# A hybrid decoder step on one core: where the sample rows land, how many input tiles wait for their store, and which tiles hold the weights of the first gate/up pass

## The chip, the cores and the metric

The kernel runs on one core of one Trainium2 chip. The metric is the device time of one launch in microseconds; the median of the runs shown is compared before and after.

## The reference, cut to what matters

The prompt (1024 rows of 1024) and 8 sample rows go through one layer with shared weights.

```python
h = rms_norm(x, norm1)
u, q, k, v, ga, gb = split_in(h, w_in, q_norm, k_norm)      # one input projection
y_pool = pool_mix(u_ext, pos, pool_mix_w, pool_scale)       # trailing means over 2/4/8/16 rows
y_attn = sink_attention(qb, kk, vv, mask, sinks)            # window 128, 8 heads, 2 kv heads
x = x + (sigmoid(ga) * (y_pool @ w_pool_proj) + sigmoid(gb) * (y_attn @ w_attn_proj)) @ w_out
h = rms_norm(x, norm2)
x = x + (silu(h @ w_gate) * (h @ w_up)) @ w_down            # 1024 -> 2816 -> 1024
```

Returned are x of both groups, the last 128 keys and values, and the last 15 rows of u. All of it is float32.

## The kernel before, in words

Every matmul is made of three passes of TensorE (PE): each operand is split into a high part (a cast, on ScalarE, L138 or L214) and a low part (a subtraction, on VectorE, L139 or L215), and high x high, high x low and low x high are added in PSUM. The program order within each engine is laid down ahead by a planner, which follows the order of the source text as a priority and takes what its own timeline believes to be ready; on the chip each engine, and the one queue through which SyncE (SP) issues nearly all DMAs, then runs that order without overtaking.

**Input stage.** The 1032 rows (8 sample rows first) are worked in three chunks `CH`. `norm_load` (L298) loads the rows of a chunk, `norm_stats` their sums of squares, `turn` (L335) transposes 128 columns of a chunk on PE and splits the result into `hTh`/`hTl`. Its inner function `keep` (L344) also copies the transposed piece into a tile `xT` and stores that to `xscr` in DRAM, from where the residual is read later. `xT` has six buffers; eight pieces belong to a chunk. `norm_bc` (L364) copies the row factors of a chunk (`bc1`) out of PSUM on ScalarE; `do_k`, `do_v` and `do_q` need them as soon as their matmuls are done (`kr`, L390). The sample rows stand in a tile `xs` of their own in the pool `st`. The keys have four units of 4128 bytes a partition in the pool `kp`: `Kh` and `Kl` for two key heads; half of each `Kl` is zeroed on GpSimd (POOL) at the start.

**First gate/up pass.** The feed-forward part works on halves of rows and columns with seven products instead of eight (`strassen`, L1138): products 1, 6, 2, 7, 5, 4, 3, each with an operand of activations (`c1h` to `c7l`, made by `combos`, L1049, for a quarter set s = 0 or 1) and one of weights. Block p = 0 of the weights is done twice: for s = 0 alone right after the output projection `out_proj(1, m)` (n = 0 in the last loop of the pass), while the second norm and the `combos` of s = 1 are being made, and for s = 1 alone at the end (n = 11). Between them p = 1 to 10 take both s. The seven weight operands of gate p = 0 were split earlier and lie in DRAM (`wscr`); those of up p = 0 lie there unsplit (`tscr`, or the weights themselves) and are split by `wparts` when their product is due. A product of n = 0 is 12 matmuls, one of n = 1 is 24.

Where these operands are put: `kept_gate` (L1236) places sets 0 to 4 in the `whi`/`wlo` tiles of the pool `wp` (four buffers each, shared with every other split weight, so also with `out_proj`) and sets 5 and 6 in units of the pool `u1` (28 units of 4128 bytes, which also hold `Mh`/`Ml` of the output projection and all `c` operands). `kept_up` (L1250) places raws 0 to 2 in units of `u1` and raws 3 to 6 in `wtemp` tiles (three buffers, shared with `wraw`). The fifth split of up goes to a tile of its own (pool `mw`). `wide` (L997) gives four wide tiles of 1024 columns, used by `out_proj` for `x2` and by `wblocks` (L1110) for the raw weights of p = 1 onwards. `mark["load"]` is a load behind which other loads are queued on SP: before, the raws of up p = 1 stand behind the load of up raw 2.

The two generators are run from the loop at the end of the pass:

```python
for i, _ in enumerate(chain(strassen(wblocks(wg_v, 2 * P * p) if p else kept_gate(0 if n else 5), streams, g),
                            strassen(wblocks(wu_v, 2 * P * p, mark["load"] if n == 1 else None) if p else kept_up(), streams, u_))):
    if n == 0 and i in (1, 3, 4, 5, 6, 7, 8, 9, 10):
        next(norm)
```

After the pass `down` follows: `srcs` (L1283) loads the products of gate and up back into units of `u1` (`ar`) and splits them.

Of the kernel before, what the change touches and what calls it, by code (L numbers as in the profile page):

```python
# [7 lines left out]
F32 = mybir.dt.float32  # L8
F32R = mybir.dt.float32r
# [7 lines left out]
P = 128  # L17
NS = 8
# [14 lines left out]
HALF = ((slice(0, 64), slice(64, 128)), (slice(64, 128), slice(0, 64)))  # L33
# [3 lines left out]
def hybrid_step(tc, x_prompt, x_sample, cache_k, cache_v, state_pool, norm1, w_in, q_norm, k_norm, sinks,  # L37
# [4 lines left out]
    V, A, G, T, SP = nc.vector, nc.scalar, nc.gpsimd, nc.tensor, nc.sync  # L42
# [12 lines left out]
    wp, wp_es = pool("wp")  # L55
# [86 lines left out]
    mark = {}  # L142
# [109 lines left out]
    def unit(p, name, dt=F32):  # L252
        return p.tile([P, NT], dt, tag="u", name=name)
# [14 lines left out]


    Kh = [unit(kp, f"Kh{kv}", F32R) for kv in range(2)]  # L270
    Kl = [unit(kp, f"Kl{kv}", F32R) for kv in range(2)]
    for kv in range(2):
        G.memset(Kl[kv][HALF[kv][1]].bitcast(F32), 0.0)
    VV = kvp.tile([P, 8, 4, 64], F32R, name="VV")
    st, st_es = pool("st", side="right")

# [21 lines left out]
    def norm_load(c):  # L298
        tiles = []
        if c == 0:  # L300
            xt = st.tile([NS, 1024], F32, name="xs")
            SP.dma_start(xt, x_sample[:, 0])
            tiles.append((NS, 0, xt))
        for i, b in enumerate(CB[c]):
            xt = unit(u1, "xr")
            for q in range(2):
                w = 512
                SP.dma_start(xt[:, w * q:w * q + w], x_prompt[0, b * P:(b + 1) * P, w * q:w * q + w])
            tiles.append((P, (NS if c == 0 else 0) + P * i, xt))
        return tiles  # L310
# [24 lines left out]
    def turn(c, tiles, k):  # L335
        c0, N = CH[c]
        pt = bank("pt")
        for n, off, xt in tiles:
            T.transpose(pt[:, off:off + n], xt[:n, k * P:(k + 1) * P], ident[:n, :n])
        hi, lo = hTh[k][:, c0:c0 + N], hTl[k][:, c0:c0 + N]  # L340
        turned[c, k] = (A.activation(hi, pt[:, :N], AF.Copy, scale=g1[k]),
                        V.scalar_tensor_tensor(lo, pt[:, :N], g1[k], hi.bitcast(F32), ALU.mult, ALU.subtract))

        def keep(e=A):  # L344
            xT = st.tile([P, 384], F32, tag="xT", bufs=6, name="xT")[:, :N]
            if e is A:
                A.copy(xT, pt[:, :N])
            else:
                V.tensor_copy(xT, pt[:, :N])
            SP.dma_start(xscr[:, k, c0:c0 + N], xT)  # L350

        return keep
# [11 lines left out]
    def norm_bc(c, rstd):  # L364
        c0, N = CH[c]
        pb = bank("pb")
        spread_of(c, rstd, pb)
        A.copy(bc1[:, c0:c0 + N], pb[:, :N])
# [63 lines left out]
    def do_v(ws, c):  # L432
        N, nb, o = CH[c][1], len(CB[c]), (NS if c == 0 else 0)
        b0 = CB[c][0]
        ps = group(ws, hTh, hTl, c, bank("pv"))

        def rest():
            vr = t512("vr")[:, :N]
            V.tensor_mul(vr, ps, bc_of(c))

            def token_major():
                pt = bank("pvt")
                for i in range(nb):
                    T.transpose(pt[:, i * P:(i + 1) * P], vr[:, o + i * P:o + (i + 1) * P], ident)
                if c == 0:
                    T.transpose(pt[:NS, 384:512], vr[:, :NS], ident)
                vb = VV[:, b0:b0 + nb]
                split(vb[:, :, 0:4:3], vb[:, :, 1:3], pt[:, :nb * P].rearrange("p (b g d) -> p b g d", g=2, d=64))
                if c == 0:
                    V.tensor_copy(vst, pt[:NS, 384:512])  # L450
                    SP.dma_start(new_v_sample[0, :, 127].rearrange("b h d -> b (h d)"), vst)
                if CB[c][-1] == 7:
                    nv = t512("nv")[:, :P]
                    V.tensor_copy(nv, pt[:, (nb - 1) * P:nb * P])
                    SP.dma_start(new_v_prompt[0, 0].rearrange("t h d -> t (h d)"), nv)

            tick()
            defer(token_major)

        return rest  # L460
# [59 lines left out]
        wv = wsplit2(rv, V)  # L520
    with behind(0, 7):
        norm_bc(0, rs[0])
    ev = do_v(wv, 0)
    ek()
    ev()
# [336 lines left out]
    raw = wraw()  # L862
# [131 lines left out]
        XG.append(p.tile([P, 2, KD, NQ], F32, name=f"xg{s}"))  # L994
        acc.append(p.tile([P, 2, NQ], F32, name=f"acc{s}"))

    def wide(name):  # L997
        return mw.tile([P, 1024], F32, tag="raw", bufs=4, name=name)

    def out_proj(s, m):  # L1000
        ws = wload(wo_v, 0, 8, P * m)
# [75 lines left out]
    def chain(*gens):  # L1077
        for g in gens:
            yield from g
# [19 lines left out]
    def wparts(src):  # L1099

        if nth[0] is None:
            return wsplit(src, 4)
        nth[0] += 1
        return wsplit(src, 4) if nth[0] % 5 else wsplit(src, 4, p=mw, bufs=1)

    def wtemp(name):
        return wp.tile([P, 4, P], F32, tag="wraw", bufs=3, name=name)
# [125 lines left out]


    norm = chain(norm_scale(1), combos(1, hc[1]))
    def kept_gate(early):  # L1236

        for i in range(7):
            if i < early:
                r = [wp.tile([P, 4, P], F32R, tag=t, bufs=4, name=t) for t in ("whi", "wlo")]  # L1240
                for a in range(2):
                    SP.dma_start(r[a].bitcast(F32), wscr[i][:, a])
                yield r
            else:
                u = unit(u1, "wk", F32R)
                SP.dma_start(u[:, :1024].bitcast(F32), wscr[i].rearrange("p a k c -> p (a k c)"))
                u = u[:, :1024].rearrange("p (a k c) -> p a k c", a=2, k=4)
                yield u[:, 0], u[:, 1]

    def kept_up():  # L1250
        for i, (kh, m) in enumerate(((0, 0), (0, 0), (1, 0), (0, 0), (0, 0), (0, 0), (1, 1))):
            raw = unit(u1, "wk")[:, :512].rearrange("p (k c) -> p k c", k=4) if i < 3 else wtemp("wk")
            load = SP.dma_start(raw, tscr[i] if i in tscr else wu_v[:, 4 * kh:4 * kh + 4, P * m:P * m + P])
            if i == 2:
                mark["load"] = load
            yield wparts(raw)

    for n, (p, streams) in enumerate([(0, [0])] + [(p, [0, 1]) for p in range(1, 11)] + [(0, [1])]):
        g = Gate()
        u_ = Up(g)  # L1260
        for i, _ in enumerate(chain(strassen(wblocks(wg_v, 2 * P * p) if p else kept_gate(0 if n else 5), streams, g),
                                    strassen(wblocks(wu_v, 2 * P * p, mark["load"] if n == 1 else None) if p else kept_up(), streams, u_))):
            if n == 0 and i in (1, 3, 4, 5, 6, 7, 8, 9, 10):
                next(norm)
        if n == 0:
            for _ in norm:
                pass
        save(p, g.g, slice(streams[0], streams[-1] + 1))
        if n == 1:
            m0_es.close()  # L1270
            xb_es.close()
            m1, m1_es = pool("m1", bufs=16, side="right")
            mt[0] = m1
# [162 lines left out]
    a = {}  # L1436
# [56 lines left out]
```

## Time and profile before

| what | before |
|---|---|
| median of 3 runs | 1282.99 us (1282.97 to 1284.46) |
| profiled execution | 1284.43 us |
| its span in the trace | 1282.7 us |
| PE busy | 1248.0 us, 97% |
| VectorE (DVE) busy | 817.3 us, 64% |
| ScalarE (ACT) busy | 501.4 us, 39% |
| mean DMA rate | 120 GB/s |

A busy share of 97% says that PE is what the span is made of; what is left to find are the few stretches in which it stands, and those in which its clock is granted at half. PE, PEld, DVE, ACT, POOL are engines, SPq is the queue on which SP issues DMAs. In rows of the timeline the bracket at the end is the idle time of the engine before the instruction, with what ended it.

### The profile page before, as it was taken

The page shows a single profiled execution, that of the slowest core. Times are in us where ns is not written, and L with a number is a line of the kernel's source. Part 1 is how long each engine was busy: PE and PEld are TensorE (multiplying, and loading weights), DVE is VectorE, ACT ScalarE, POOL GpSimd, SP SyncE. Part 2 cuts the span into 40 slices and gives each one's busy share as a digit, 9 for nine tenths or more (in the row PEclk, how much of TensorE's full clock was granted, in tenths as well). Part 3 has the DMA queues.
Part 4 walks back from the last instruction along what each step waited for, and adds up shares of the span by engine and source line. Part 5 has one row for each costly group of instructions (what it writes and reads, how often), then busy time and mean ns, then how long its engine had stood idle before and what let it go on. Part 6 is the DMA issues. An engine that isn't in the chain of part 4 may idle for free.

```text
span 1282.7 us, 23784 instructions
## 1 busy us (share of the span) xinstructions
PE 1248.0 (97%) x9436; PEld 1233.9 (96%) x9436; DVE 817.3 (64%) x1600; ACT 501.4 (39%) x980; POOL 55.9 (4%) x193
## 2 busy tenths in 40 slices
PE   5999999999999999996999999999999999999997
PEld 5999999999999999996999999999999999999997
DVE  5769788585353484487756566665666566878642
ACT  5747555451233234454323232232322234334433
POOL 3213211000000000000000000000000000000000
PEclk7999999999999999998999999999999999999999
DMA  7411101211244125664232323322232668847404
GB/s 241 132 46 51 42 23 53 73 51 51 74 157 123 42 83 158 175 187 164 79 125 83 91 87 113 108 93 91 84 124 75 210 222 293 290 156 240 147 26 125
DMA packets 149166, 153.50 MB, mean 120 GB/s; under 512 B 15207, under 2 KB 116263, under 8 KB 149031
## 3 DMA queue, kind: packets, MB, share of 16 engines
q1 hardware_dynamic: 148959, 150.71, 37.1%
q8 instruction: 74, 1.21, 0.4%
q0 software_dynamic: 96, 1.27, 0.2%
q14 instruction: 37, 0.30, 0.1%
HBM read 114.02 MB, written 39.20 MB: 119 GB/s over the span
## 4 chain that ended last, share of the span: by engine, by line
PE 93%; DMA 4%; DVE 2%; SPq 0%; ACT 0%; issue 0%; ACTq 0%; DVEq 0%
PE py L1132 5%; PE py L1134 5%; PE py L1133 5%; PE pg L211 5%; PE pg L209 5%; PE pg L210 5%; PE pz L1132 3%; PE pz L1133 3%; PE px L1134 3%; PE pz L1134 3%; PE px L1132 3%; PE px L1133 3%; PE dy L1132 2%; PE pw L209 2%; PE dy L1133 2%; PE dy L1134 2%
## 5 line engine op out<-in xcount | busy, mean ns | idle before, releaser
L209 PE MATMUL pg<-hTh,whi 128*128 128x384 f32 (+1 forms) x384 | 123.6, 322 | 0.0
L210 PE MATMUL pg<-hTl,whi 128*128 128x384 f32 (+1 forms) x384 | 123.3, 321 | 0.0
L211 PE MATMUL pg<-hTh,wlo 128*128 128x384 f32 (+1 forms) x384 | 122.9, 321 | 0.0
L139 DVE TENSOR_TENSOR wlo<-wraw,whi 128x512 fp32r<-128x512 f32 x102 | 70.1, 687 | 69.6 <-ACT whi L138 62.3
L138 ACT CAST whi<-wraw 128x512 fp32r<-128x512 f32 x102 | 63.0, 619 | 131.2 <-PE pa L210 31.3
L138 ACT CAST whi<-t 128x512 fp32r<-128x512 f32 x80 | 49.4, 621 | 153.8 <-PE py L1133 79.0
L138 ACT CAST whi<-raw 128x512 fp32r<-128x512 f32 x60 | 37.3, 621 | 114.7 <-PE px L1133 66.0
L1132 PE MATMUL dy<-ah,whi 128*128 128x258 f32 x264 | 75.1, 285 | 0.0
L1133 PE MATMUL dy<-al,whi 128*128 128x258 f32 x264 | 75.0, 284 | 0.0
L1134 PE MATMUL dy<-ah,wlo 128*128 128x258 f32 x264 | 74.8, 284 | 0.0
L209 PEld LDWEIGHTS pg<-hTh,whi 128*128 128x128 f32 x384 | 72.6, 189 | 0.6 <-DVE t L823 0.2
L210 PEld LDWEIGHTS pg<-hTl,whi 128*128 128x128 f32 x384 | 72.6, 189 | 0.5
L211 PEld LDWEIGHTS pg<-hTh,wlo 128*128 128x128 f32 x384 | 72.4, 189 | 0.3
L209 PE MATMUL pw<-mh,whi 128*128 128x258 f32 x256 | 72.4, 283 | 0.0
L210 PE MATMUL pw<-ml,whi 128*128 128x258 f32 x256 | 72.1, 282 | 0.0
L211 PE MATMUL pw<-mh,wlo 128*128 128x258 f32 x256 | 72.0, 282 | 0.0
L139 DVE TENSOR_TENSOR wlo<-raw,whi 128x512 fp32r<-128x512 f32 x60 | 41.0, 684 | 35.7 <-ACT whi L138 30.7
L138 ACT CAST whi<-H 128x512 fp32r<-128x512 f32 x55 | 33.8, 620 | 69.0 <-PE dy L1133 23.0
L215 DVE TENSOR_TENSOR al<-ar,ah 128x1032 fp32r<-128x1032 f32 (+1 forms) x42 | 47.9, 1140 | 16.0 <-ACT ah L214 16.0
L139 DVE TENSOR_TENSOR wlo<-t,whi 128x512 fp32r<-128x512 f32 x80 | 54.0, 683 | 3.2 <-ACT whi L138 3.2
L1132 PE MATMUL px<-c1h,whi 128*128 128x258 f32 x172 | 49.3, 286 | 6.1 <-ACT whi L138 6.0
L139 DVE TENSOR_TENSOR wlo<-H,whi 128x512 fp32r<-128x512 f32 x55 | 37.5, 688 | 21.5 <-ACT whi L138 20.4
(446 smaller groups left out, 4451.7 us busy)
## 6 DMA issues: line engine op xcount, KB each, us to landing
ar<-s SPq DMA_DIRECT2D x35, 516.0 KB
d<-in_w_down_dram SPq DMA_DIRECT2D x44, 256.0 KB
s<-g SPq DMA_DIRECT2D x40, 258.0 KB
wraw<-in_w_in_dram SPq DMA_DIRECT2D x40, 256.0 KB
raw<-in_w_gate_dram SPq DMA_DIRECT2D x20, 512.0 KB
raw<-in_w_up_dram SPq DMA_DIRECT2D x20, 512.0 KB
wraw<-in_w_out_dram SPq DMA_DIRECT2D x32, 256.0 KB
s<-fs SPq DMA_DIRECT2D x30, 258.0 KB
```

What stands on the lines that cost most here:

```text
L138: mark["act"] = A.copy(hi, raw)
L139: mark["dve"] = e.tensor_sub(lo, raw, hi.bitcast(F32))
L209: T.matmul(ps, lhsT=wh, rhs=xh, start=(k == 0), stop=False)
L210: T.matmul(ps, lhsT=wh, rhs=xl, start=False, stop=False)
L211: T.matmul(ps, lhsT=wl, rhs=xh, start=False, stop=(k == n - 1))
L215: e.tensor_sub(lo, src, hi.bitcast(F32))
L1132: T.matmul(ps, lhsT=wh, rhs=ah, start=start, stop=False, skip_group_check=True)
L1133: T.matmul(ps, lhsT=wh, rhs=al, start=False, stop=False, skip_group_check=True)
L1134: T.matmul(ps, lhsT=wl, rhs=ah, start=False, stop=stop, skip_group_check=True)
```

## The change

The sample rows `xs` are loaded into a unit of `kp`, the one that the second key head's low part `Kl1` will take; `Kl1` is made (and its half zeroed on POOL) only after the turn of chunk 0. `xT` has eight buffers instead of six. All loads of the first gate/up pass are written out ahead of its loop, in order of need (gate sets 0 to 6, then up raws 0 to 6). Gate sets 0 to 2 stay in `whi`/`wlo`, sets 3 and 4 go to wide tiles, sets 5 and 6 to units. Up raws 0 to 2 go to the small `wtemp` tiles, raws 3 to 6 to units. `mark["load"]` is now the last of these loads, and the gate raws of p = 1 stand behind it too, not only the up raws. In the last pass (n = 11) all seven gate sets and all seven up raws go to units.

```diff
     Kh = [unit(kp, f"Kh{kv}", F32R) for kv in range(2)]
-    Kl = [unit(kp, f"Kl{kv}", F32R) for kv in range(2)]
-    for kv in range(2):
-        G.memset(Kl[kv][HALF[kv][1]].bitcast(F32), 0.0)
+    Kl = []
+
+    def low_keys():
+        Kl.append(unit(kp, f"Kl{len(Kl)}", F32R))
+        G.memset(Kl[-1][HALF[len(Kl) - 1][1]].bitcast(F32), 0.0)
+
+    low_keys()
...
         if c == 0:
-            xt = st.tile([NS, 1024], F32, name="xs")
-            SP.dma_start(xt, x_sample[:, 0])
+            xt = unit(kp, "xs")[:NS]
+            SP.dma_start(xt[:, :1024], x_sample[:, 0])
...
-            xT = st.tile([P, 384], F32, tag="xT", bufs=6, name="xT")[:, :N]
+            xT = st.tile([P, 384], F32, tag="xT", bufs=8, name="xT")[:, :N]
...
     with behind(0, 7):
         norm_bc(0, rs[0])
+    low_keys()
     ev = do_v(wv, 0)
...
-    def wide(name):
-        return mw.tile([P, 1024], F32, tag="raw", bufs=4, name=name)
+    def wide(name, dt=F32):
+        return mw.tile([P, 1024], dt, tag="raw", bufs=4, name=name)
...
-    def kept_gate(early):
-
+    def gate_set(i, where):
+
+        if where == "w":
+            r = [wp.tile([P, 4, P], F32R, tag=t, bufs=4, name=t) for t in ("whi", "wlo")]
+            for a in range(2):
+                SP.dma_start(r[a].bitcast(F32), wscr[i][:, a])
+            return r
+        u = unit(u1, "wk", F32R)[:, :1024] if where == "u" else wide("wk", F32R)
+        mark["load"] = SP.dma_start(u.bitcast(F32), wscr[i].rearrange("p a k c -> p (a k c)"))
+        u = u.rearrange("p (a k c) -> p a k c", a=2, k=4)
+        return u[:, 0], u[:, 1]
+
+    def up_raw(i, small):
+        kh, m = ((0, 0), (0, 0), (1, 0), (0, 0), (0, 0), (0, 0), (1, 1))[i]
+        raw = wtemp("wk") if small else unit(u1, "wk")[:, :512].rearrange("p (k c) -> p k c", k=4)
+        mark["load"] = SP.dma_start(raw, tscr[i] if i in tscr else wu_v[:, 4 * kh:4 * kh + 4, P * m:P * m + P])
+        return raw
+
+    def kept_gate(first):
         for i in range(7):
...
+            yield first[i] if first else gate_set(i, "u")
+
+    def kept_up(first):
+        for i in range(7):
+            yield wparts(first[i] if first else up_raw(i, False))
+
+    first_gate = [gate_set(i, w) for i, w in enumerate("wwwbbuu")]
+    first_up = [up_raw(i, i < 3) for i in range(7)]
...
-        for i, _ in enumerate(chain(strassen(wblocks(wg_v, 2 * P * p) if p else kept_gate(0 if n else 5), streams, g),
-                                    strassen(wblocks(wu_v, 2 * P * p, mark["load"] if n == 1 else None) if p else kept_up(), streams, u_))):
+        for i, _ in enumerate(chain(strassen(wblocks(wg_v, 2 * P * p, mark["load"] if n == 1 else None) if p else kept_gate(None if n else first_gate), streams, g),
+                                    strassen(wblocks(wu_v, 2 * P * p, mark["load"] if n == 1 else None) if p else kept_up(None if n else first_up), streams, u_))):
```

## Rows read from the trace of the kernel before

**Rows 1.** The page: busy time and share of the span, by engine.

```profile
PE 1248.0 (97%) x9436; PEld 1233.9 (96%) x9436; DVE 817.3 (64%) x1600; ACT 501.4 (39%) x980; POOL 55.9 (4%) x193
```

**Rows 2.** Waits of PE, first 60 us: total, times, longest.

```profile
PE pkt L397 <- DVE kr L390: 6.2, 1, 6.2
```

**Rows 3.** The chain that ended last, 22 to 27 us: start, us, what.

```profile
22.24 3.12 DMA xscr<-xT
...
25.70 0.40 ACT bc L368
...
26.12 0.45 DVE kr L390
```

**Rows 4.** Timeline of ACT and DVE, 20 to 26 us: start, us, instruction.

```profile
20.16 0.62 ACT L180 CAST qwh<-qw 128x512 fp32r<-128x512 f32 x1 [1.14 <-DMA qw<-in_w_in_dram]
24.96 0.85 ACT L347 COPY xT<-pt 128x264 f32<-128x264 f32 x2 [4.18 <-DMA xscr<-xT]
...
20.81 0.69 DVE L181 TENSOR_TENSOR qwl<-qw,qwh 128x512 fp32r<-128x512 f32 x1 [1.06 <-ACT qwh L180]
```

**Rows 5.** Stretches: length; busy of PE, PEld, DVE, ACT, POOL; granted clock, DMA, GB/s.

```profile
20.40:26.60 6.20, 0.02 (x1) 0.00 (x0) 1.14 (x3) 1.42 (x4) 0.00 (x0) 0.66 0.88 303
26.60:32.70 6.10, 6.09 (x28) 5.72 (x29) 4.17 (x12) 4.22 (x9) 2.95 (x15) 0.51 0.46 124
```

**Rows 6.** Timeline of POOL: one zeroed half, and the idle time after the first norm.

```profile
4.93 0.95 POOL L273 MEMSET Kl<- 64x1032 f32 x1
...
28.53 0.20 POOL L117 TENSOR_SCALAR rstdk<-rs_v 128x4 int32<-128x4 int32 x1 [15.56 <-DVE rs_v L131]
```

**Rows 7.** Waits of PE, 565 to 620 us: total, times, longest.

```profile
PE px L1132 <- ACT whi L138: 5.4, 1, 5.4
PE pb L1039 <- DVE dg L1034: 2.0, 1, 2.0
```

**Rows 8.** Stretches of the first gate/up pass, 570 to 613 us; columns as in Rows 5.

```profile
570.00:613.00 43.00, 30.81 (x216) 28.72 (x214) 31.99 (x50) 18.76 (x28) 0.00 (x0) 0.88 0.52 171
578.00:588.00 10.00, 6.82 (x61) 6.33 (x60) 3.64 (x15) 2.92 (x4) 0.00 (x0) 1.00 1.03 344
593.00:613.00 20.00, 11.78 (x74) 10.85 (x74) 20.00 (x27) 11.81 (x18) 0.00 (x0) 0.83 0.20 66
601.00:606.00 5.00, 3.96 (x17) 3.64 (x18) 5.00 (x8) 1.82 (x4) 0.00 (x0) 0.50 0.35 108
```

**Rows 9.** Timeline of DVE, 585 to 613 us.

```profile
585.53 0.43 DVE L1164 TENSOR_TENSOR g<-py,g 128x258 f32<-128x258 f32 x1 [1.79 <-PE py L1134]
...
603.01 1.28 DVE L139 TENSOR_TENSOR wlo<-wk,whi 128x512 fp32r<-128x512 f32 x2
...
612.36 0.68 DVE L139 TENSOR_TENSOR wlo<-raw,whi 128x512 fp32r<-128x512 f32 x1
```

**Rows 10.** The chain that ended last, 577 to 584 us: start, us, what.

```profile
577.90 6.08 DMA wlo<-w
```

**Rows 11.** Timeline of PE: first and last matmul of the up pass's last two products.

```profile
615.76 0.28 PE L1132 MATMUL py<-c4h,whi 128*128 128x258 f32 x1
...
618.76 0.28 PE L1134 MATMUL pz<-c3h,wlo 128*128 128x258 f32 x1
```

**Rows 12.** Timeline of SP's queue: a raw of p = 1, an up raw, the down stage's first.

```profile
575.97 0.38 SPq L1114 DMA_DIRECT2D raw<-in_w_gate_dram  x1
...
583.30 0.32 SPq L1253 DMA_DIRECT2D wk<-t  x1
...
1019.33 0.32 SPq L1287 DMA_DIRECT2D ar<-s  x1
```

**Rows 13.** Waits of SP's queue, 535 to 630 us: total, times, longest.

```profile
SPq L1253 <- DVE xg L1067: 19.2, 1, 19.2
```

**Rows 14.** The page's DMA issues: count and size of one.

```profile
raw<-in_w_gate_dram SPq DMA_DIRECT2D x20, 512.0 KB
```

**Rows 15.** Timeline of ACT: cast of the last up raw of the last pass.

```profile
1032.75 0.62 ACT L138 CAST whi<-wk 128x512 fp32r<-128x512 f32 x1
```

More of the change, by code (lines that the diff above doesn't have):

```diff
@@ L1235, in hybrid_step @@
     norm = chain(norm_scale(1), combos(1, hc[1]))
-    def kept_gate(early):
-        for i in range(7):
[L1239 to L1256, printed above, removed]
+    def gate_set(i, where):
[14 more added lines that the diff above has]
+    def kept_gate(first):
+        for i in range(7):
+            yield first[i] if first else gate_set(i, "u")
[4 more added lines that the diff above has]
+    first_up = [up_raw(i, i < 3) for i in range(7)]
     for n, (p, streams) in enumerate([(0, [0])] + [(p, [0, 1]) for p in range(1, 11)] + [(0, [1])]):
```

## The prediction, made before the changed kernel was run

> **What bounds the kernel now.** The page first: PE is busy for 97% of the span [rows 1], so the reader should look for stretches in which PE stands or is granted half its clock. The waits of PE and the table of stretches give two places that this change touches.
>
> The first is the input stage. From 20.4 to 26.6 us PE does nothing: the transposes of the keys wait 6.2 us for `kr` on DVE [rows 2]. The chain tells whom `kr` waited for [rows 3]: for `bc`, a copy on ACT, which stood behind two `xT` copies, and those behind a store of an earlier `xT` that landed at 22.24 + 3.12 = 25.36 us. The timeline of ACT shows the same from the other side: 4.18 us idle, ended by that store [rows 4]. Six buffers, eight pieces to a chunk: pieces 7 and 8 wait for a store that travels among the loads of x (DMA share 0.88 in this stretch). When PE starts again its granted clock is 0.51, the lower of its two levels, 1.2 GHz, nearly up to 32.7 us [rows 5].
>
> The second is the first gate/up pass, 570 to 613 us: PE is busy for 30.8 of 43.0 us, so idle for 12.2 [rows 8], with one wait of 5.4 us for the cast of the up pass's first weights [rows 7]. Two limits follow each other there. At 578 to 588 us the DMA engines are full (1.03, 344 GB/s). From 593 to 613 us nothing is loaded to speak of, and DVE has not a microsecond free (20.00 of 20.00): it makes the s = 1 operands, while the up splits and the additions stand between them [rows 8]. What ends the stretch is a DVE split, that of the first weights of p = 1, at 612.36 + 0.68 = 613.0 us [rows 9].
>
> **Input stage, term A.** With eight buffers all pieces of chunk 0 have one, so both copies run at once after their turn and `bc` no longer stands behind the store. What is late next: on ACT the two casts of `qwh`, the last at 20.16 + 0.62 = 20.78 us, and on DVE the subtraction that ends at 20.81 + 0.69 = 21.50 us [rows 4]. If the order stays, `kr` runs at 21.5 to 21.95 us (0.45, rows 3) and PE goes on at 22.0 instead of 26.6 us: 4.6 us less. The upper end is the whole wait, 6.2 us, if the planner puts `bc` ahead of the casts. The lower end is 1.5 us, if the wait only moves to the copies of chunk 1 (second rival).
> The slow clock afterwards cost 6.1 x (1 - 0.51) = 3.0 us [rows 5]. Whether 1.6 us of idle time still brings it about the trace does not show for this place. The nearest rows are short waits in the gate pass, where 2.0 us [rows 7] lie in the stretch at full clock (578 to 588 us, 1.00), while the stretch behind the 5.4 us wait has 0.50 [rows 8]; short waits can therefore go either way. I take half, 1.5 us, with ends 0 and 3.0. A = 4.6 + 1.5 = 6.1 us. From 30 to 570 us PE has no other wait of this size, so the gain stays in the total.
>
> At nothing: the zeroing of `Kl1`, 0.95 us on POOL, moves from 4.93 us behind the first norm, where POOL idles for 15.56 us [rows 6]; without that cover it would cost its 0.95 us. The load of the sample rows keeps its place and size; its unit is free again once they are turned.
>
> **Gate/up pass, term B.** Three effects, in order.
> (1) Gate sets 3 and 4 no longer need the tiles that the output projection holds. Before, the set of product 7 took 6.08 us to land, at 583.98 us [rows 10]; its product ended late, and DVE, in order, stood 1.79 us before the addition behind it [rows 9] with the rest of the second norm queued there. With the set in place the norm of s = 1, and so DVE's full stretch, starts 1.8 us sooner.
> (2) Up raws 0 to 2 now have small tiles that the output projection frees early, and the `whi` tiles that sets 3 and 4 gave up; raw 3 follows. So four splits can run while DVE is busy for 3.64 of 10 us [rows 8], ahead of the full stretch. A split there takes 1.28 / 2 = 0.64 us [rows 9]: 4 x 0.64 = 2.6 us leave it.
> (3) The up products no longer wait behind DVE. Products 4 and 3 of up, 24 matmuls that came after 613 us, starts 3.0 us apart from first to last with one foreign matmul between [rows 11], or 24 x 0.12 = 2.9 us, are done in time that PE spent idle.
> B = 1.8 + 2.6 + 2.9 = 7.3 us. The low end is effect (1) alone, 1.8 us. The high end is all idle time, 12.2 us, and the half clock of 601 to 606 us, 3.96 x 0.5 = 2.0 us, less the 2.0 us for `dg` that the norm keeps [rows 7, 8]: 12.2 us.
>
> Each queue passed: on SP the gate raws of p = 1, before at 575.97 us, now stand behind the last up raw. Units for six operands come free when the output projection's operands are read; the last up load of before that needed no further unit left at 583.30 us [rows 12]. Add one slow load, 6.1 us [rows 10]: about 590 us, and the split that needs it comes at 613 (613 - 7.3 in the forecast). The cover is over 15 us. Without it: before, SP stood 19.2 us for one up raw's unit [rows 13], until 602.8 us; the raws of p = 1 would land at 608.9, their split end near 610, and B falls from 7.3 to about 5.8.
>
> The last pass (n = 11) asks for four more units than before, just when the down stage wants its first. I cost it at nothing, since the gate sets give back seven units first; the fifth rival has its price.
>
> **Sum.** 6.1 + 7.3 = 13.4 us. Against the profiled execution (1284.43 us, span 1282.7) that is 1271.0; this execution lies 1.44 us above the median of the runs shown, so the median after should be 1282.99 - 13.4 = 1269.6 us.
>
> **The rivals.**
> 1. Bytes decide in the gate pass. DMA stands at 1.03 of its share at 578 to 588 us, so a new order of loads brings nothing, and only the two raws of p = 1 that leave the stretch help: 2 x 512 KB [rows 14] at 344 GB/s = 3.0 us [rows 8]. B = 3.0, sum 9.1: 1273.9 us. For it: that share; against it: before 570 us there is room, and the wide tiles and small tiles open there. The Trainium skill speaks for this rival: "DMA: Bandwidth & Descriptors", section "Issuing engines are not separate DMA queues", says that all DMAs run on the same 16 engines and interleave; by it the sets, pulled forward against each other, only trade places.
> 2. The store's wait moves. Chunk 1's pieces need the buffers of chunk 0 back, whose stores still land from 25.4 us on [rows 3]. If the planner sets the ninth copy ahead of what PE needs, A is 1.5: 8.8 in all, 1274.2 us.
> 3. Both places give their high end: A = 6.2 + 3.0, B = 12.2, 21.4 in all: 1261.6 us.
> 4. It doesn't do what it says: the planner leaves `bc` and the up casts where they are, other waits take over, and the time stays at 1283 us.
> 5. Slower: the down stage starves. If its first load, `ar`, gets a unit only after the last up raw of the last pass is split, it leaves not at 1019.33 us but at 1032.75 + 0.62 + 0.68 = 1034.05 us [rows 9, 12, 15], 14.7 us later. If the stage cannot catch up, PE stands for that and then runs 2.0 us longer at half clock [rows 8]: 16.7 - 13.4 = 3.3 us more than before, 1286.3 us. It decides from about 1030.7 us on (11.4 us late). Against it: the seven gate units are given back one product at a time before that.
>
> **How the numbers follow.** Chances: forecast 0.49, rival 1 0.17, rival 2 0.10, rival 3 0.11, rival 4 0.06, rival 5 0.07. The forecast's own spread is 1265 to 1274. The range runs from rival 3 (1261.6, rounded to 1261) to both low ends together, 1283 - 1.5 - 1.8 = 1279.7, say 1279.5; it leaves out rivals 4 and 5 and a little beside them. A measurement of this kernel tells a change from none at about 0.2%, 2.6 us. Faster by more: forecast and rivals 1 to 3, 0.87; within it 0.06; slower 0.07.
>
> **What the profile after would show.** Right: no wait of PE for `kr` above 2 us and no wait of ACT for `xscr<-xT` before `bc`; in the gate pass four up splits ahead of the multiplication of `xg`, no 5 us wait of `px` for `whi`, and the first p = 1 split on DVE some 13 us earlier than 613 us. Wrong: the wait stands at another copy of `xT`; SP stands long before a load of `wk` or of p = 1; DVE's full stretch is as long as before and PE waits at its end; `dx` waits for `ar`. The forecast fails most easily in effect (3), which needs the planner to put the up products before the operands of s = 1 on PE.

## The result, and the profile after

| what | before | after |
|---|---|---|
| median | 1282.98 us (1282.86 to 1284.46, 4 runs) | 1273.17 us (1270.72 to 1274.98, 4 runs) |
| profiled execution, span | 1284.43 us, 1282.7 us | 1270.72 us, 1268.7 us |
| ratio of the medians | | 0.9919, 95% interval 0.9908 to 0.9931 |

The changed kernel takes 9.8 us less; by the ratio 10.4 us (8.9 to 11.8). A second set of its runs, on another occasion, gave 1273.76 us and 0.9928 (0.9913 to 0.9944). The forecast was 1269.6 us, range 1261 to 1279.5: inside, but 3.6 us too hopeful.

To see where the time went, the start of one and the same matmul is compared in both traces; each number is how many us earlier it starts than before. "Before", "after", "input part" and so on are one profiled execution each.

| landmark (before) | after | after, second profile | input part alone | pass part alone | place of xs alone |
|---|---|---|---|---|---|
| `pk`, first (12.24) | -1.85 | -2.26 | -2.27 | -1.16 | -1.67 |
| `pkt`, first (26.61) | 4.22 | 3.33 | 3.35 | -0.50 | -0.43 |
| `pb` of chunk 1 (39.97) | 6.78 | 6.07 | 6.08 | 0.36 | 0.84 |
| `pg`, first (173.00) | 6.68 | 6.00 | 5.91 | 0.39 | 0.80 |
| `pa`, first (281.86) | 8.25 | 6.01 | 5.92 | 1.94 | 2.38 |
| `pw`, last (577.39) | 8.69 | 6.27 | 6.47 | 2.49 | 1.63 |
| `px` of p = 2, first (650.56) | 11.61 | 6.66 | 6.93 | 4.46 | 1.56 |
| `dx`, first (1041.27) | 12.25 | 7.30 | 7.13 | 5.04 | 1.46 |
| `po`, last (1278.19) | 13.98 | 7.96 | 8.37 | 6.57 | 2.15 |

The input stage gives 5.9 to 6.7 us. Between `pg` and `pa`, where nothing was changed, an execution gains another 1.5 us or none (last section). From the last `pw` to the first `px` of p = 2, the first gate/up pass, the two profiles of the changed kernel gain 2.9 and 0.4 us. From there to the end come 0.6 to 2.4 us more, in kernels without a change there too (1.4 us with the input part alone, 0.6 with the place of xs alone), so they are not counted.

**Input stage.** The waits of PE in the first 45 us after (total, times, longest), the stretches of [rows 5] (the first one from 20.00 us on), and ACT in the timeline:

```profile
PE pt L343 <- DMA xs<-in_x_sample_dram: 3.7, 1, 3.7
...
PE pk L209 <- ACT whi L138: 1.1, 1, 1.1
```

```profile
20.00:26.60 6.60, 6.60 (x55) 6.26 (x54) 5.64 (x16) 4.37 (x10) 1.86 (x10) 1.00 0.94 323
26.60:32.70 6.10, 6.10 (x44) 5.92 (x42) 4.65 (x12) 5.14 (x12) 3.24 (x17) 1.00 0.51 138
```

```profile
20.65 0.62 ACT L180 CAST qwh<-qw 128x512 fp32r<-128x512 f32 x1 [1.10 <-DMA qw<-in_w_in_dram]
21.17 0.38 ACT L351 COPY xT<-pt 128x264 f32<-128x264 f32 x1
21.44 0.39 ACT L372 COPY bc<-pb 128x264 f32<-128x264 f32 x1
...
27.51 0.89 ACT L351 COPY xT<-pt 128x384 f32<-128x384 f32 x2 [1.20 <-DMA xscr<-xT]
```

The wait for `kr` [rows 2] is gone: `bc` runs at 21.44 us behind a copy that waited for no store, PE has no gap from 20 us on, and the clock stays at 1.00 where it was 0.51 [rows 5]. The store is still waited for, now by a copy of chunk 1 and for 1.20 us, and no wait of PE answers to it. The first line has grown: PE stands 3.7 us for the sample rows, before it was 0.7. In return the wait of `pk` for the cast of the key weights fell from 3.8 to 1.1 us. The rows' load left SP second before; after, it leaves fifth, behind three loads of x:

```profile
1.25 1.31 SPq L312 DMA_DIRECT2D xr<-in_x_prompt_dram  x3
2.61 0.33 SPq L306 DMA_DIRECT2D xs<-in_x_sample_dram  x1
```

**First gate/up pass.** The stretches of [rows 8] after, the stretch from 568 to 580 us, and the waits of PE from 560 to 645 us:

```profile
570.00:613.00 43.00, 33.67 (x249) 32.23 (x247) 37.70 (x65) 19.16 (x29) 0.00 (x0) 0.92 0.45 143
578.00:588.00 10.00, 7.00 (x41) 6.60 (x41) 8.85 (x16) 2.27 (x4) 0.00 (x0) 0.83 0.64 192
593.00:613.00 20.00, 14.99 (x106) 14.16 (x104) 20.00 (x33) 9.31 (x14) 0.00 (x0) 0.91 0.24 65
...
568.00:580.00 12.00, 8.67 (x81) 8.47 (x79) 7.64 (x22) 6.12 (x11) 0.00 (x0) 1.00 1.04 356
```

```profile
PE pb L1044 <- DVE dg L1039: 3.8, 1, 3.8
PE px L1137 <- ACT c5h L214: 2.5, 1, 2.5
PE px L1137 <- ACT g L1159: 2.1, 1, 2.1
```

PE's 5.4 us for the first up cast [rows 7] are gone, and the full stretch of the DMA engines lies some 10 us earlier; 8.7 of these are the ones by which the whole pass starts sooner. But PE waits 3.8 instead of 2.0 us for `dg`, and DVE is still full for 20.00 of 20.00 us. DVE's timeline shows what stands ahead of the multiplication of `xg`, with which its full stretch begins:

```profile
575.15 0.16 DVE L131 TENSOR_SCALAR rs_v<-pst 86x6 f32<-86x6 f32 x1 [1.19 <-PE pst L1035]
...
576.87 0.69 DVE L139 TENSOR_TENSOR wlo<-wk,whi 128x512 fp32r<-128x512 f32 x1 [0.96 <-DMA wk<-in_w_up_dram]
...
577.89 0.68 DVE L139 TENSOR_TENSOR wlo<-wk,whi 128x512 fp32r<-128x512 f32 x1
...
579.66 0.69 DVE L1039 TENSOR_TENSOR dg<-ident,rstd 86x516 f32<-86x516 f32 x1
580.46 0.69 DVE L1123 TENSOR_TENSOR t<-raw 128x512 f32<-128x512 f32 x1
581.99 0.69 DVE L1124 TENSOR_TENSOR t<-raw,t 128x512 f32<-128x512 f32 x1 [0.84 <-DMA raw<-in_w_gate_dram]
582.60 0.68 DVE L1128 TENSOR_TENSOR t<-raw 128x512 f32<-128x512 f32 x1
583.20 4.64 DVE L1048 TENSOR_TENSOR xg<-xg,pb 128x1032 f32<-128x1032 f32 x4
```

Two up splits and three sums of p = 1 stand inside the norm's chain, and two of them wait for loads that land in the full stretch of the DMA engines. In the kernel before, the same chain had none of them:

```profile
582.39 0.16 DVE L131 TENSOR_SCALAR rs_v<-pst 86x6 f32<-86x6 f32 x1 [2.74 <-PE pst L1030]
...
588.63 4.65 DVE L1043 TENSOR_TENSOR xg<-xg,pb 128x1032 f32<-128x1032 f32 x4 [1.29 <-PE pb L1039]
```

From the end of the last `pw` matmul (577.67 and 568.99 us), `xg` starts after 11.0 us before and 14.2 us after: 3.2 us later, although the weights of product 7 and of the up pass are there sooner.

### The profile page after: what moved, and what is told of

It reads as the page before. It is cut to its first block, busy times and chain, and to the rows that moved or that the text cites. A ratio compares the mean times of both kernels' runs of the same rounds, so it can differ in the third digit from the quotient of the medians.

```text
span 1268.7 us, 23785 instructions
## 1 busy us (share of the span) xinstructions
PE 1244.1 (98%) x9436; PEld 1229.2 (97%) x9436; DVE 815.5 (64%) x1600; ACT 501.5 (40%) x980; POOL 55.4 (4%) x193
## 4 chain that ended last, share of the span: by engine, by line
PE 92%; DVE 3%; DMA 3%; ACT 1%; issue 1%; SPq 0%; ACTq 0%; DVEq 0%
PE pg L211 5%; PE pg L209 5%; PE pg L210 5%; PE py L1137 5%; PE py L1138 5%; PE py L1139 5%; PE px L1137 3%; PE px L1139 3%; PE pz L1139 3%; PE pz L1138 3%; PE pz L1137 3%; PE px L1138 3%; PE dy L1137 2%; PE dy L1138 2%; PE dy L1139 2%; PE pw L209 2%
## 5 line engine op out<-in xcount | busy, mean ns | idle before, releaser
L139 DVE TENSOR_TENSOR wlo<-wraw,whi 128x512 fp32r<-128x512 f32 x102 | 70.1, 687 | 71.7 <-ACT whi L138 58.6
L209 PE MATMUL pw<-mh,whi 128*128 128x258 f32 x256 | 72.4, 283 | 0.0
L214 ACT CAST ah<-ar 128x1032 fp32r<-128x1032 f32 (+1 forms) x42 | 41.2, 982 | 26.0 <-DMA ar<-s 26.0
```

The lines of the kernel that those rows point to most:

```text
L139: mark["dve"] = e.tensor_sub(lo, raw, hi.bitcast(F32))
L209: T.matmul(ps, lhsT=wh, rhs=xh, start=(k == 0), stop=False)
L214: A.copy(hi, src)
```

## The experiments

The pass is compared by three times, each counted from the end of the last `pw` matmul in the profile of that run; "median" is of the timed runs, "ratio" against the kernel before in the same set.

| run | `rs_v` | `xg` | `px` of p = 2 | median us | ratio [95%] |
|---|---|---|---|---|---|
| before | 4.7 | 11.0 | 72.9 | 1282.98 | 1 |
| e1_input | 4.7 | 10.5 | 72.4 | 1274.98 | 0.9942 [0.9930, 0.9954] |
| e3_xs_only | 4.7 | 10.3 | 73.0 | 1283.34 | 1.0004 [0.9993, 1.0014] |
| after | 6.2 | 14.2 | 70.0 | 1273.17 | 0.9919 [0.9908, 0.9931] |
| a2_again | 6.4 | 15.2 | 72.5 | 1273.76 | 0.9928 [0.9913, 0.9944] |
| e2_pass | 6.2 | 15.1 | 70.9 | 1281.10 | 0.9983 [0.9974, 0.9992] |
| e5_xs_t0 | 6.2 | 15.4 | 72.6 | 1273.58 | 0.9917 [0.9902, 0.9932] |
| e4_behind | 6.2 | 10.8 | 69.1 | 1271.55 | 0.9916 [0.9903, 0.9928] |
| e8_up_units | 4.7 | 11.9 | 69.1 | 1272.82 | 0.9916 [0.9895, 0.9937] |
| e9_pool | 6.2 | 12.8 | 69.8 | 1271.57 | 0.9902 [0.9884, 0.9919] |
| e11_no_lo | 6.2 | 13.0 | 69.7 | 1271.08 | 0.9909 [0.9893, 0.9926] |
| e12_half_sets | 7.2 | 13.0 | 69.7 | 1272.77 | 0.9911 [0.9895, 0.9927] |
| e7_no_wide | 4.9 | 11.6 | 71.8 | 1275.80 | 0.9933 [0.9917, 0.9949] |
| e13_units_behind | 4.7 | 14.0 | 71.7 | 1276.14 | 0.9944 [0.9930, 0.9957] |

### The two parts apart

The input part alone: the hunks of the diff on `Kl`, `xs` and `xT`, in the kernel before.

> The input stage's part of the change alone (sample rows in a key unit, eight xT buffers), the gate/up pass as before. Theory: the trace of the changed kernel stands 8.1 us ahead at the first matmul of the output projection, all of it from the input stage and the clock behind it; so this kernel is 8.1 us faster than before, about 1275, with the pass and the tail unmoved. Rival: the input stage gives only the 4.2 us by which the transposes of the keys came earlier, and the rest is the clock of single executions: then about 1279.

It gave 1274.98 us: by the ratio 7.4 us (5.9 to 9.0). The time is the one that the theory named, but not the share of 8.1 us: this run's profile stands 5.9 us ahead at `pg` and 6.5 at the last `pw`. The rest of the 8.1 was the 1.5 us that the first profile of the changed kernel gained between `pg` and `pa`. The forecast's 6.1 us for this stage lies in the interval.

The pass part alone: the changed kernel with those hunks taken back.

> The gate/up pass's part alone, the input stage as before. Theory: the pass stands 3.5 us ahead by the first product of p = 2 (11.6 ahead, of which 8.1 from the input stage) and the down stage adds up to 2.3 us through the last pass's places: 3.5 to 5.8 us faster, 1277 to 1279.5. Rival: the prediction's size for this part, 7.3 us, hidden in the full change by something else: then about 1275.7.

By the ratio 2.2 us (1.0 to 3.3), against 7.3 forecast; theory and rival were both too hopeful. The two parts add up to 9.6 us, beside 10.4 and 9.2 for the whole. So the forecast's surplus lies in the pass.

The place of the sample rows alone, in the kernel before:

```diff
-            xT = st.tile([P, 384], F32, tag="xT", bufs=8, name="xT")[:, :N]
+            xT = st.tile([P, 384], F32, tag="xT", bufs=6, name="xT")[:, :N]
```

(against the run of the input part)

> The sample rows in a key unit, but xT still with six buffers, the pass as before. Theory: the gain of the input stage is the two buffers alone, and moving the sample rows costs about 1.9 us at the start, since their load now leaves SP behind three loads of the prompt (first key matmul 14.1 instead of 12.2 us): PE still waits some 4 to 6 us for kr, and the time is 1283 to 1285. Rival: the new place itself changes the order on ACT, and the wait is gone with six buffers too: about 1276.

1.0004: no difference. Its waits of PE show the old one back beside the new one:

```profile
PE pkt L401 <- DVE kr L394: 3.7, 1, 3.7
PE pt L343 <- DMA xs<-in_x_sample_dram: 3.6, 1, 3.6
```

Behind that wait the clock is 0.72 from 26.6 to 32.7 us, with eight buffers 1.00. The gain of the stage, the clock's part included, is that of the two buffers.

### The sample rows' load early again

```diff
-            xt = unit(kp, "xs")[:NS]
+            xt = unit(t0p, "xs")[:NS]
```

> The whole change, but the sample rows are loaded into a unit of the pool t0p, so that no later key waits on them and their load need not come behind the three loads of xr. Theory: in the changed kernel that load leaves SP fifth, at 2.61 us instead of 1.25, and this is why the keys of chunk 0 start 1.85 us later (14.09 instead of 12.24 us). Put back, it leaves second, the wait of 3.7 us of the transposes for the rows goes, pk starts near 12.3 us, and the whole input stage gains 1.2 to 1.9 us more: about 1271.5 us. Rival: the keys are bound by something else on their way (the copies of xT on ACT, kr), so that what is won at 12 us is lost again by 22 us: pkt starts at 22.4 us as in the changed kernel, and the time stays at 1273.2 us.

The rival came true. The wait for the rows shrank to 0.6 us and another took its place:

```profile
PE pk L209 <- ACT whi L138: 3.9, 1, 3.9
```

`pk` started at 13.29 instead of 14.09 us, and `pkt` at 22.70 instead of 22.39. What PE waits for next is the key weights' cast and then `kr`, and `kr` (22.22 us here, 21.91 after) stands behind the second cast of `qw`, which starts when its load has landed, at 20.95 us here and 20.65 after. So the late load of the rows costs nothing that can be measured.

### What stands ahead of the second norm

The sums of p = 1 and the splits of up raws 3 to 6 held on DVE behind the multiplication:

```diff
-            V.tensor_mul(x, x, pb[:, t, :NQ].unsqueeze(1).broadcast_to([P, 4, NQ]))
+            mark["xg"] = V.tensor_mul(x, x, pb[:, t, :NQ].unsqueeze(1).broadcast_to([P, 4, NQ]))
...
-        V.tensor_sub(t1, b12, b11)
-        V.tensor_sub(t2, b22, t1)
+        with tc.issue_after(mark["xg"].ins):
+            V.tensor_sub(t1, b12, b11)
+            V.tensor_sub(t2, b22, t1)
...
-        V.tensor_sub(t3, b22, b12)
+        with tc.issue_after(mark["xg"].ins):
+            V.tensor_sub(t3, b22, b12)
...
-            yield wparts(first[i] if first else up_raw(i, False))
+            with tc.issue_after(mark["xg"].ins) if first and i > 2 else nullcontext():
+                w = wparts(first[i] if first else up_raw(i, False))
+            yield w
```

> The full change, and on DVE the three subtractions of p = 1 and the splits of up raws 3 to 6 held behind the multiplication of xg for s = 1. Theory: in the full change these operations stand inside the second norm's chain (two splits, one of them waiting 0.96 us, and three subtractions, one waiting 0.84 us), so xg starts 14.5 us after the output projection's last matmul, before 11.2; held back, it starts 3 us sooner, and PE's wait for dg falls from 3.8 to about 1.7 us; the kernel gains 1 to 3 us on the full change. Rival: DVE is full from there on whatever the order, so what leaves the chain comes back behind it: the time stays at that of the full change within 1 us.

`xg` starts 10.8 us after the last `pw`, as in the kernel before, and the pass takes 69.1 us, with one later run the shortest of all. Against the first profile of the changed kernel `xg` wins 3.4 us and the pass 0.9: the rest comes back, as the rival had it, as waits for the splits that were held:

```profile
PE pb L1044 <- DVE dg L1039: 2.0, 1, 2.0
PE px L1141 <- DVE wlo L139: 1.9, 1, 1.9
PE pz L1141 <- DVE wlo L139: 1.8, 1, 1.8
```

The time, 1271.55 us, can't be told from that of the changed kernel.

The changed kernel again, beside the next three runs:

> The changed kernel once more, on the chip of the three runs after it. Both theories: 1271 to 1275 us. The stretch from the last matmul of pw to the 145th of px took 72.9 us before, 70.0 us in the first profile of the changed kernel and 72.6 us in a run whose instructions have the same order in that stretch. If the stretch varies that much by itself, it comes out between 70 and 72.6 us here; if the 70.0 us belong to the kernel, within 0.5 us of it.

The pass took 72.5 us here and 70.0 us in the first profile, with every instruction in the same order. The loads differ: `rs_v` came 0.3 us later, the first of the two splits in the chain ended at 581.0 - 571.4 = 9.6 instead of 8.6 us after the last `pw`, `pb` waited 4.6 instead of 3.8 us, and the clock fell:

```profile
580.00:590.00 10.00, 6.06 (x26) 5.72 (x27) 8.55 (x17) 1.29 (x3) 0.00 (x0) 0.66 0.58 185
```

(second profile of after, columns as in [rows 5]; the first one has 0.83 in this stretch). Over the 70 us behind the last `pw` the clock is 0.95 in the first profile and 0.90 in the second; the two other runs with this order agree (0.95 with 70.9 us in e2_pass, 0.90 with 72.6 us in e5_xs_t0). So one profile of this pass is good to some 2.5 us, no better, and differences below that are read here from the order of the work and from the timed runs.

The low parts of up splits 3 to 6 left out:

```diff
+        if not low:
+            return hi, hi
         mark["dve"] = e.tensor_sub(lo, raw, hi.bitcast(F32))
...
```

> The changed kernel without the low parts of the first pass's up splits 3 to 6: four DVE subtractions of 0.64 us are left out, and the matmuls take the high part in their place. No byte of the loads and no matmul goes. Theory (DVE's work sets the end of the first gate/up pass): the pass is 2.0 to 2.6 us shorter, in all some 2 us less than the changed kernel beside it. Rival (the landing of its operands sets it, since the DMA engines are full from 568 to 580 us and two steps of the second norm's chain wait for loads there): the splits stand behind that point, and the pass moves by less than 0.7 us.

The gate sets 3 to 6 loaded by half:

```diff
+        a = 1 if first_pass[0] else 2
-        mark["load"] = SP.dma_start(u.bitcast(F32), wscr[i].rearrange("p a k c -> p (a k c)"))
+        mark["load"] = SP.dma_start(u[:, :512 * a].bitcast(F32), wscr[i][:, :a].rearrange("p a k c -> p (a k c)"))
...
-        return u[:, 0], u[:, 1]
+        return u[:, 0], u[:, a - 1]
...
```

> The changed kernel, where the gate sets 3 to 6 of the first pass are loaded by their high half alone (256 instead of 512 KB each, 1 MB less in all) and the matmuls take the high half twice. DVE's work stays. Theory (DVE's work sets the end of the pass): the waits of the chain for loads (0.96 and 0.84 us ahead of the multiplication of xg) go, which starts up to 2 us sooner, but the work behind it is the same, so the pass gains 0 to 2 us. Rival (bytes set it, the first rival of the forecast): 1 MB at 344 GB/s is 3.0 us, and the whole of it shows at the end of the pass, 3 us less than the changed kernel beside it.

These two were to part DVE's work from the bytes, and they did not: each moves `xg` to 13.0 us and the pass to 69.7 us, beside 72.5 in their set and 71.5 on average over the four profiles with the changed kernel's order (70.0, 72.5, 70.9, 72.6). One reason is that each edit also changed the planner's order. Without the low parts the chain runs through as in the kernel before (`dg` 8.8 us after the last `pw`; 9.0 before, 10.7 in the changed kernel), but one sum of p = 1 stands ahead of `xg` and waits for its load:

```profile
583.53 0.69 DVE L1125 TENSOR_TENSOR t<-raw 128x512 f32<-128x512 f32 x1 [2.88 <-DMA raw<-in_w_gate_dram]
```

With the half sets two up splits run ahead of `rs_v`, which comes at 7.2 us. By the medians they are 2.7 and 1.0 us below the changed kernel beside them, with overlapping intervals. The forecast's first rival, by which the bytes alone decide, asked for 3 us; that is not excluded, but the run that holds the sums and splits behind `xg` speaks against it: it loads the same bytes in the same order in this stretch and has the shortest pass.

### Moving work off DVE

The sums of p = 1 and the low parts of up raws 3 to 6 on GpSimd (`e = G` in `wblocks` and `wsplit`), with the rows' load early.

> As the run before, and in the first gate/up pass the sums of weight blocks of p = 1 and the low parts of the up splits 3 to 6 are made by GpSimd instead of DVE. Theory: DVE's work sets the length of the pass, so what leaves its full stretch shortens it: three sums of the gate part and four low parts, about 7 x 0.6 = 4.2 us of DVE; with what GpSimd adds in latency some 2 to 4 us less than the run before: 1268 to 1270 us. Rival: what sets the length is the order (the chain sum of squares, rs_v, dg, pb, xg) and not the amount of DVE's work; then the multiplication of xg starts about 2 us sooner (no sums ahead of it) but the end of the pass moves by less than 1 us, or GpSimd, being slower, keeps PE waiting for the low parts: 1271 to 1274 us.

1271.57 us: in the rival's range, and 2.0 us less than the run of the section before, whose rows stand in the same place (1273.58 us), the low end of what the theory asked for; the intervals overlap, so this decides nothing. The pass took 69.8 us. The edit moves eight sums, those of gate and up, and four low parts, twelve operations and not the seven of the expectation. Still DVE was not relieved: in the 69 us behind the last `pw` it is busy for 51.1 us, against 50.1 in the run with the same place of the rows, because its own instructions grew longer beside GpSimd's. DVE first, then POOL:

```profile
587.98 2.32 DVE L1063 TENSOR_TENSOR s<-xg 128x1032 f32<-128x1032 f32 x1
590.22 0.41 DVE L1164 TENSOR_TENSOR ut<-py,us 128x258 f32<-128x258 f32 x1
...
590.89 1.66 DVE L1069 TENSOR_TENSOR xg<-xg 128x1032 f32<-128x1032 f32 x1
```

```profile
587.92 1.29 POOL L139 TENSOR_TENSOR wlo<-wk,whi 128x512 fp32r<-128x512 f32 x1 [1.87 <-ACT whi L138]
589.36 2.09 POOL L139 TENSOR_TENSOR wlo<-wk,whi 128x512 fp32r<-128x512 f32 x1 [0.15 <-ACT whi L138]
```

`s<-xg` takes 1.22 us in the changed kernel, 2.32 here: it began 0.06 us after POOL's and ended 1.09 us after it. POOL's next one waited in turn. `ut<-py,us`, which reads PSUM, kept its 0.41 us. The Trainium skill says the same: "SBUF — State Buffer", section "SBUF: two separate sides", has one pair of ports that VectorE and GpSimd share as an exclusive lock for the whole instruction, where VectorE has two inputs in SBUF and GpSimd reads SBUF. These rows agree with it: 2.32 us instead of 1.22 and, on GpSimd, 2.09 instead of 1.29.

### The tiles

Gate sets 3 and 4 in `whi`/`wlo` again, not in wide tiles:

```diff
-    first_gate = [gate_set(i, w) for i, w in enumerate("wwwbbuu")]
+    first_gate = [gate_set(i, w) for i, w in enumerate("wwwwwuu")]
```

> The whole change, but the gate sets 3 and 4 stand in whi/wlo tiles as before, not in the wide ones; up raws 0 to 2 keep their small tiles. Theory: the wait for product 7's set (6.08 us before) was not what held the pass, as DVE's work decides: the pass keeps 2 of its 2.6 to 3.5 us, in all 1273 to 1274.5 us. Rival: early sets were what let PE reach the up products in its idle time; without them the wait of PE comes back and the pass's whole gain is gone: 1276 to 1277 us.

71.8 us and 1275.80 us: between theory and rival, 1.8 us longer than the first profile of the changed kernel and within its spread. `xg` starts early (11.6 us), yet the pass is long; its longest wait is `px` of p = 1 for the copy on ACT, 4.0 us, and ACT stood behind a cast that waited 7.00 us for a sum on DVE:

```profile
612.83 0.62 ACT L138 CAST whi<-t 128x512 fp32r<-128x512 f32 x1 [7.00 <-DVE t L1124]
613.35 0.58 ACT L1159 COPY g<-px 128x516 f32<-128x516 f32 x1
```

The changed kernel has the same pair with 3.94 us. The wide tiles may be worth 1 to 2 us; these runs don't settle it.

Up raws 0 to 2 in units, 3 to 6 in small tiles:

```diff
-    first_up = [up_raw(i, i < 3) for i in range(7)]
+    first_up = [up_raw(i, i > 2) for i in range(7)]
```

> The whole change, but with the tiles of the up raws exchanged: 0 to 2 in the large units, as before the change, and 3 to 6 in the small ones. The gate sets stay as changed. Theory: the early up splits stand in the chain of the second norm (rs_v and dg come later by two of them); without them the multiplication of xg starts 1 to 3 us sooner, and the splits come back in the full stretch, so that the first products of n = 1 start within 1 us of where the changed kernel has them: 1272.5 to 1274.5 us. Rival: what the change gains in this pass it gains through these splits (four of 0.64 us, the second effect of the forecast); without them the pass loses 2.6 us: about 1275.8 us.

The time, 1272.82 us, is the theory's, `xg` starts 2.3 us sooner, and the pass takes 69.1 us, but not for the theory's reason: the up splits did not leave the chain. One runs ahead of it (567.67 us), and four stand between `rs_v` and `xg` (575.79 and 582.99 us):

```profile
579.63 0.69 DVE L139 TENSOR_TENSOR wlo<-wk,whi 128x512 fp32r<-128x512 f32 x1 [1.23 <-ACT whi L138]
...
580.85 0.68 DVE L139 TENSOR_TENSOR wlo<-wk,whi 128x512 fp32r<-128x512 f32 x1
...
581.78 1.28 DVE L139 TENSOR_TENSOR wlo<-wk,whi 128x512 fp32r<-128x512 f32 x2
```

What left it are the three sums of p = 1, which follow `xg` here, and product 7, which PE runs behind `pst` again: `rs_v` at 4.7 instead of 6.2 us, 1.5 of the 2.3. So this run doesn't tell what early splits are worth. The small tiles for the first up raws, on which the forecast's second effect rested, bring nothing that can be measured.

Both edits together, this one and the order of the first run of the section before:

> The changed kernel with the tiles of the up raws exchanged (0 to 2 in the large units, 3 to 6 in the small ones), and with the sums of p = 1 and the splits of the up raws 3 to 6 held on DVE behind the multiplication of xg. Each of the two alone ended this pass 0.9 us sooner than the first profile of the changed kernel. Theory (DVE is full, and an order can only move its idle time to the front): the multiplication of xg starts 11 us after the last matmul of pw instead of 14.2, and the pass ends 0 to 1 us sooner than in the changed kernel: 1272 to 1273.5 us. Rival (the start of the second norm sets the end): 3 us sooner, 1270 us.

Both expectations fell: 1276.14 us, by the medians slower than either edit alone and than the changed kernel beside it (only the interval of the first edit lies clear of this one's). Four up raws share three small tiles here, so the last one waits on SP until a split that is held on DVE gives its tile back, and all loads of p = 1 wait behind it on SP's queue. The queue's wait, and the stretch in which next to nothing is loaded (DMA 0.01, 2 GB/s):

```profile
SPq L1258 <- DVE wlo L139: 16.2, 1, 16.2
```

```profile
580.00:590.00 10.00, 7.34 (x36) 7.00 (x37) 7.72 (x13) 2.31 (x5) 0.00 (x0) 0.66 0.01 2
```

No kernel that does the whole work gave a time that is clearly below the changed kernel's. Lowest are the one that holds the sums and splits behind `xg` (1271.55 us, highest run 1273.62) and the one with work on GpSimd (1271.57 us, highest run 1273.10).

## Why the prediction was right, and where its sum was not

- **What bounds the kernel, and term A.** Right: 6.1 us forecast, 5.9 to 6.7 by the landmarks at `pg`, 7.4 (5.9 to 9.0) by the timed runs. Its two addends were both off and made up for each other. Up to `pkt` 3.3 to 4.2 us came instead of 4.6, as PE now runs 22.4 us instead of the forecast 22.0 and, in the second profile, 23.3. The clock gave back 2.6 to 2.7 us (`pkt` to `pb` of chunk 1) and not half of 3.0: there is no idle time left in front of that stretch, where the forecast had kept some. The order was the forecast one, casts, `bc`, `kr`.
- **At nothing, input stage.** The load of the sample rows did not keep its place on SP's queue (2.61 instead of 1.25 us): a tile that others reuse gets another place from the planner, and in `t0p` the rows leave second again. `pk` starts 1.9 to 2.3 us later than before, but so it does by 1.1 and 1.2 us in two runs whose rows are loaded at 1.25 us (e5_xs_t0, e2_pass), so about half of that is the execution's; nothing of it is left further on. `Kl1` did not wait for the turn, as the section on the change has it: POOL has zeroed both halves by 5.9 us (3.46 and 4.93 us, 0.95 each), and PE turns the first rows at 6.37. The cover named for it wasn't needed.
- **Term B, effect (1): the step that failed.** It had the second norm start 1.8 us sooner, and it starts 3.2 to 4.4 us later. The wait that it removed did go, but the forecast held the rest of the order fixed, and the planner changed it in two places. On PE it put product 7, now early, ahead of `pst`: `rs_v` at 6.2 instead of 4.7 us, 1.5 us. On DVE it filled the freed time with work that it held to be ready: splits whose loads had not landed, and the sums of p = 1. Each is 0.6 to 0.7 us, but they stand inside a chain of short dependent steps, where nothing hides them. With this work held back (e4_behind) the steps from `rs_v` to `dg` take 2.6 us, before 4.3: there are the 1.7 us of effect (1), and product 7 takes 1.5 of them back (`xg` at 10.8 and 11.0 us).
- **Effects (2) and (3).** Five splits of up run ahead of `xg` or in its chain, where one did before: four more, as forecast. And up's products run in PE's idle time: the first up product starts 584.45 - 568.99 = 15.5 us after the last `pw` instead of 600.80 - 577.67 = 23.1. Where `xg` starts as before, the pass is 72.8 - 69.1 = 3.7 us shorter (e4_behind; 72.8 is the mean of the three profiles with the old pass). Only three splits stand ahead of `xg` in that run, two more than before, but the run with five (e8_up_units) takes 69.1 us too. That is what the two are worth by the profiles, and not 2.6 + 2.9 = 5.5; that later work of p = 1 fills DVE up again (20.00 of 20.00 us) is the likely reason, and only argued.
- **The sum of B.** The timed runs of the pass alone give 2.2 us (1.0 to 3.3) in place of 7.3. By the profiles (2) and (3) bring 3.7 us, of which 72.8 - 71.5 = 1.3 are left in the changed kernel's order, so the late norm costs 2.4 us; by the two of these four profiles with the better clock (70.0 and 70.9 us) it costs 1.4. The timed runs don't confirm a size: the ratio with the chain cleared is 0.9916, those of the changed kernel's order 0.9917 to 0.9928, 0.1 to 1.5 us apart with overlapping intervals. That the norm is late and why is shown; what it costs in time stays open.
- **Rows misread.** The split at 612.36 us [rows 9] was called the first of p = 1. It is the second; the first stands at 606.84 us before and at 595.35 after. The expected 13 us for it are therefore no test. And the 2.0 us wait [rows 7] was taken for one that leaves the clock at full; it ends at 587.48 us, and from 588 to 593 us the clock before is 0.66.
- **Gate raws of p = 1 behind the mark.** They were expected at about 590 us and priced at nothing for being early enough. They land at 580.5 to 582 us; being early was no cover but the trouble, since DVE takes their sums at once. A kernel without the mark was not run.
- **Rivals.** The first named 3.0 us for B and 1273.9 us, nearest of all to what came; its reason, bytes, is one part of the late norm (waits of 0.96 and 0.84 us for loads) and not shown to be the whole, and the two raws of p = 1 that were to leave the full stretch are loaded in its second half, so its nearness is in part luck. The second, whose 1.5 us has no working, was seen in form (1.20 us of ACT, a copy of chunk 1 that waits for a store) at no cost. The fifth did not happen: the down stage's first matmul is as far ahead as the gate/up passes before it (12.25 us, and 11.97 at the 601st `px`).
- **Chances.** The likeliest single value was too low since all three effects of B were summed at their own size in one queue order; the wide range held it, and the forecast's own spread, 1265 to 1274, just so.

## What to carry to other kernels

Work that is filled into an engine's idle time delays what follows if the idle time is inside a dependent chain: look for what follows the gap before counting it as free. Where buffers run short for a store that travels among loads, a few more can be worth much: two of them gave 5.9 to 6.7 us here, with the clock behind the wait. Before a small gain is read from one profile of each kernel, compare two profiles of the same one.

## What the runs showed of the chip that was not expected

**The clock falls without idle time.** In the attention stage, right behind a run of matmuls of 8 columns (`pY<-pz,cv`), PE is busy throughout, and yet one profile of the changed kernel is granted 0.64 there, part of the time at the lower level of 1.2 GHz, and the other 1.00. First the second profile, then the first (columns as in [rows 5]):

```profile
230.00:234.00 4.00, 4.00 (x21) 3.72 (x21) 1.89 (x10) 1.87 (x10) 0.00 (x0) 0.64 0.20 73
```

```profile
230.00:234.00 4.00, 4.00 (x26) 3.87 (x26) 2.65 (x11) 2.20 (x12) 0.00 (x0) 1.00 0.19 74
```

It costs 1.56 us (the second profile is 0.67 us behind the first at 230 us and 2.23 at 233 us). The profile of before has the slow one too, as have nine of the other thirteen; in the first profile of the changed kernel, e2_pass, e3_xs_only and e5_xs_t0 the clock stays at 1.00. What decides it no run shows. This is the step of 1.5 us between `pg` and `pa` in the first table: of the 14.0 us between the two profiled spans, these are not the change's.
